# Nine shared fp32 slots, hardware-queue loads and ScalarE casts in a Winograd convolution

## The chip, the cores and the metric

The kernel runs on one core of a Trainium2 chip. The metric is the device time of one execution, in microseconds (us), lower is better. Each number of the form "128.61 us" is the median over several executions. Some executions of the kernel before are slower; an execution more than 1.5% above the fastest of its kernel is called slow, and comparisons use fast executions only. The profile is one fast execution; its span, from the first to the last instruction, is about 2 us shorter than the time of the same execution (125.7 and 127.53 us for the kernel before). In the profile PE is TensorE (matmuls), DVE is VectorE, ACT is ScalarE, POOL is GpSimd, and SP issues the transfers of the sync queue; DMA stands for the sixteen engines that move data between HBM, the large memory, and SBUF, the core's own. PSUM is the memory that the matmuls write to.

## The reference, cut to what matters

A 3x3 convolution, stride 1, padding 1, fp32: 16 images of 64 channels, 64x64 points, to 128 channels.

```python
def setup_inputs():
    batch, c_in, h, w, c_out = 16, 64, 64, 64, 128
    return {"x": np.random.randn(batch, c_in, h, w).astype(np.float32),
            "weight": np.random.randn(c_out, c_in, 3, 3).astype(np.float32) * 0.1}
# reference: x padded by 1; output[b, co] += weight[co, ci, kh, kw] * x_pad[b, ci, kh:kh+h, kw:kw+w]
```

x is 16.8 MB, the output 33.6 MB. All of it must pass through HBM once.

## The kernel before: the parts that matter

Two images (2 x 64 channels) make one "pair" of 128 partitions; there are eight pairs. One pair is 2 MB of fp32 coming in and 2 x 2 MB going out. Along the rows the kernel uses a small Winograd scheme: per block of 16 output rows there is one shared product group U (over sums of two neighbouring rows, `ss`), and two groups A and B (over the rows themselves, `xs`). VectorE adds U to A and to B and so writes the output tiles `ot`. The matmuls want fp16.

```python
    xpool = ctx.enter_context(tc.tile_pool(name="xpool", bufs=5))    # fp16 input pairs, 8 KB a partition
    opool = ctx.enter_context(tc.tile_pool(name="opool", bufs=8))    # fp32 output images, 16 KB
    ...
    nc.sync.dma_start(w_raw, w_flat)
    x0 = opool.tile([128, H, W], F32, tag="ot", name="x0")
    for lo, hi in cuts:                                              # pair 0 comes as fp32, in four pieces
        nc.sync.dma_start(x0[:, lo:hi, :], x_rows[0:128, lo:hi, :])
    ...
    def load(p):                                                     # pairs 1 to 7: the DMA casts to fp16
        xs[p] = xpool.tile([128, H, W], F16, tag="xs", name="xs")
        keep(nc.gpsimd.dma_start(xs[p], x_rows[128 * p : 128 * p + 128, :, :]))
    ...
    for p in range(NP):
        if p + 1 < NP:
            for lo in (0, 16):
                sums(nc.gpsimd, p + 1, xs[p + 1], lo, 16)            # ss of the next pair, on POOL
        ...
        for blk in range(4):
            ...
            U = group([(G1, None)])
            for b2 in range(2):
                keep(nc.scalar.copy(ut, U[b2]))                      # ScalarE: PSUM -> SBUF
            A = group([(G21, 1), (G0, -1)])
            for b2 in range(2):
                nc.vector.tensor_add(ots[b2][:, j0 : j0 + RB, 0, :], A[b2], us[b2])
            Bt = group([(G01, 0), (G2, 2)])
            ...                                                      # the same for the odd rows
            # after block 3 of a pair (pair 7: after blocks 1 and 3): two stores on the sync queue
```

## Time and profile before

| | before |
|---|---|
| time, median of all | 128.61 us (128.06 to 132.51; the last is slow) |
| span of the profile | 125.7 us |
| PE busy | 107.0 us |
| last matmul of the chain of waits ends | 111.84 us |
| HBM read + written | 17.07 + 33.55 = 50.62 MB |
| last data packet ends | 124.3 us |

Lines of the profile's page of the kernel before. The rows under "busy" have one digit for each fortieth of the span (9 = 90% or more busy); GB/s counts bytes after the cast; the queue lines are packets, MB and share of the sixteen DMA engines' time.

```profile
PE 107.0 (85%) x978; PEld 55.9 (44%) x978; DVE 83.7 (67%) x134; ACT 40.8 (32%) x72; POOL 34.8 (28%) x28
...
PE   0489799999999999999999999999999999990000
...
DMA  4999999999999999999999999999999999999980
...
q1 hardware_dynamic: 3312, 35.95, 68.5%
q0 software_dynamic: 1008, 7.34, 28.5%
q8 instruction: 7, 0.11, 0.3%
...
HBM read 17.07 MB, written 33.55 MB: 403 GB/s over the span
```

Three stretches of the same trace, from the view by windows. The columns are start:end, length, then busy time and number of instructions for each engine, then the granted TensorE clock, the DMA share and the GB/s.

```profile
12.00:24.00 12.00, 11.15 (x103) 5.66 (x101) 9.79 (x16) 5.03 (x9) 8.42 (x4) 1.00 1.03 216
...
72.00:88.00 16.00, 16.00 (x154) 8.46 (x152) 12.50 (x21) 5.37 (x10) 4.20 (x2) 1.00 1.01 429
...
96.00:104.00 8.00, 8.00 (x78) 4.25 (x76) 6.67 (x11) 2.15 (x4) 0.00 (x0) 1.00 1.01 430
```

Two engines are full at once here: PE and the DMA. PE's work ends at about 112 us and the transfers go on to 124 us (the end of the last data packet in the trace). From 12 to 24 us only casting loads run (but for the end of pair 0's last piece, which lands at 12.5 us): 216 GB/s of fp16 written is about 432 GB/s of fp32 read. From 72 us on only stores run, at 429 GB/s to 88 us.

### The profile page before, as it was taken

The page shows a single profiled execution, that of the slowest core. Times are in us where ns is not written, and L with a number is a line of the kernel's source. Part 1 is how long each engine was busy: PE and PEld are TensorE (multiplying, and loading weights), DVE is VectorE, ACT ScalarE, POOL GpSimd, SP SyncE. Part 2 cuts the span into 40 slices and gives each one's busy share as a digit, 9 for nine tenths or more (in the row PEclk, how much of TensorE's full clock was granted, in tenths as well). Part 3 has the DMA queues.
Part 4 walks back from the last instruction along what each step waited for, and adds up shares of the span by engine and source line. Part 5 has one row for each costly group of instructions (what it writes and reads, how often), then busy time and mean ns, then how long its engine had stood idle before and what let it go on. Part 6 is the DMA issues. An engine that isn't in the chain of part 4 may idle for free.

```text
span 125.7 us, 2408 instructions
## 1 busy us (share of the span) xinstructions
PE 107.0 (85%) x978; PEld 55.9 (44%) x978; DVE 83.7 (67%) x134; ACT 40.8 (32%) x72; POOL 34.8 (28%) x28
## 2 busy tenths in 40 slices
PE   0489799999999999999999999999999999990000
PEld 0334355555555555555555555555555555540000
DVE  0180798778877777877787778777877787773000
ACT  4283833333333333324333333333333333330000
POOL 2710297893029201930930093000000000000000
PEclk9999999999999999999999999999999999999755
DMA  4999999999999999999999999999999999999980
GB/s 130 325 353 216 224 214 222 211 182 331 326 305 362 315 315 323 422 321 326 307 409 443 433 427 438 417 422 433 427 433 438 417 422 433 427 417 422 422 370 34
DMA packets 4330, 43.43 MB, mean 345 GB/s; under 512 B 480, under 2 KB 480, under 8 KB 1120
## 3 DMA queue, kind: packets, MB, share of 16 engines
q1 hardware_dynamic: 3312, 35.95, 68.5%
q0 software_dynamic: 1008, 7.34, 28.5%
q8 instruction: 7, 0.11, 0.3%
q14 instruction: 3, 0.02, 0.0%
HBM read 17.07 MB, written 33.55 MB: 403 GB/s over the span
## 4 chain that ended last, share of the span: by engine, by line
PE 77%; DMA 8%; ACT 2%; SPq 1%; DVE 1%; issue 1%; DVEq 0%
PE acc L140 77%; DMA x<-in_x_dram 8%; SPq L46 1%; ACT ut L154 1%; ACT xs L94 1%; DVE ot L158 1%; DVEq L195 0%; DVE ot L161 0%; SPq L42 0%; DVEq L158 0%
## 5 line engine op out<-in xcount | busy, mean ns | idle before, releaser
L140 PE MATMUL acc<-xs,Wt 64*128 64x504 f16 (+3 forms) x768 | 95.1, 379 | 0.8 <-ACT ut L154 0.7
L140 PEld LDWEIGHTS <-Wt 64*128 64x128 f16 x960 | 54.8, 96 | 52.4 <-issue 5.1
L158 DVE TENSOR_TENSOR ot<-acc,ut 128x512 f32<-128x512 f32 x64 | 41.2, 686 | 21.2 <-PE acc L140 18.0
L154 ACT COPY ut<-acc 128x512 f32<-128x512 f32 x64 | 34.2, 589 | 64.1 <-issue 59.6
L161 DVE TENSOR_TENSOR ot<-acc,ut 128x512 f32<-128x512 f32 x64 | 41.1, 685 | 0.0
L69 POOL TENSOR_TENSOR ss<-xs 128x1024 f16<-128x1024 f16 x14 | 29.5, 2125 | 23.1 <-DMA xs<-in_x_dram 9.3
L140 PE MATMUL acc<-ss,Wt 64*128 64x504 f16 (+1 forms) x192 | 32.5, 384 | 0.9 <-DVE ss L69 0.9
L69 DVE TENSOR_TENSOR ss<-x 128x512 f16<-128x512 f32 x4 | 2.8, 690 | 9.6 <-DMA x<-in_x_dram 9.6
L56 POOL DMA_DIRECT2D xs<-in_x_dram x7 | 4.0, 575 | 15.8 <-PE acc L140 15.8
L87 PE MATMUL wp<-ident,w 128*64 128x128 f16 x18 | 1.3, 328 | 4.5 <-POOL w L50 4.5
L94 ACT CAST xs<-x 128x1024 f16<-128x1024 f32 (+2 forms) x4 | 4.1, 1052 | 2.4 <-DMA x<-in_x_dram 2.4
L87 PEld LDWEIGHTS <-w 128*64 128x64 f16 x18 | 1.1, 209 | 4.5 <-POOL w L50 4.5
L89 ACT ACT_TABLE_LOAD x1 | 1.3, 1283 | 0.7 <-PEq L184 0.7
L89 ACT CAST Wt<-wp 128x384 f16<-128x384 f32 x1 | 0.5, 480 | 3.1 <-PE wp L87 3.1
L50 POOL CAST w<-w_raw 128x576 f16<-128x576 f32 x1 | 0.7, 662 | 2.5 <-DMA w_raw<-in_weight_dram 2.5
L96 ACT CAST Wt<-wp 128x384 f16<-128x384 f32 x1 | 0.5, 479 | 0.5 <-DVE Wt L92 0.5
L91 DVE TENSOR_TENSOR Wt<-wp,Wt 128x384 f16<-128x384 f32 x1 | 0.6, 550 | 0.0
L92 DVE TENSOR_TENSOR Wt<-wp,Wt 128x384 f16<-128x384 f32 x1 | 0.5, 548 | 0.0
L97 ACT CAST Wt<-wp 128x384 f16<-128x384 f32 x1 | 0.5, 485 | 0.0
masks.py:199 POOL TENSOR_SCALAR_AFFINE_SELECT ident<-ident 128x128 f16<-128x128 f16 x1 | 0.3, 292 | 0.1
masks.py:197 POOL MEMSET ident<- 128x128 f16 x1 | 0.2, 204 | 0.3 <-POOLq L184 0.3
L184 POOL MEMSET const-float32-0.0<- 128x1 f32 x1 | 0.1, 98 | 0.2 <-issue 0.2
(3 smaller groups left out, 0.3 us busy)
## 6 DMA issues: line engine op xcount, KB each, us to landing
out_dram<-ot SPq DMA_DIRECT2D x14, 2048.0 KB, 18.1
xs<-in_x_dram POOLq DMA_DIRECT2D x7, 1024.0 KB, 15.4
out_dram<-ot SPq DMA_DIRECT2D x4, 1024.0 KB, 10.2
x<-in_x_dram SPq DMA_DIRECT2D x2, 512.0 KB, 6.0
x<-in_x_dram SPq DMA_DIRECT2D x1, 576.0 KB, 4.7
x<-in_x_dram SPq DMA_DIRECT2D x1, 448.0 KB, 9.9
w_raw<-in_weight_dram SPq DMA_DIRECT2D x1, 288.0 KB, 3.0
```

The source lines that it names most:

```text
L46: nc.sync.dma_start(x0[:, lo:hi, :], x_rows[0:128, lo:hi, :])
L50: keep(nc.gpsimd.tensor_copy(w16, w_raw))
L56: keep(nc.gpsimd.dma_start(xs[p], x_rows[128 * p : 128 * p + 128, :, :]))
L69: eng.tensor_add(ss[p][:, lo : lo + n, :], v[:, lo : lo + n, 0, :], v[:, lo : lo + n, 1, :])
L87: nc.tensor.matmul(wp[q : q + 64, k * CO : k * CO + CO], w16[:, t::9], ident)
L89: keep(nc.scalar.copy(wrow(G1), wps[1]))
L91: keep(nc.vector.tensor_sub(wrow(G21), wps[2], wrow(G1)))
L94: keep(nc.scalar.copy(xs[0][:, lo:hi, :], x0[:, lo:hi, :]))
L140: nc.tensor.matmul(tiles[b2][:, lo - j0 : hi - j0, c_lo:c_hi], Wt[p0 : p0 + 64, wi, kw, :], rhs, start=i == 0, stop=i == n - 1,)
L154: keep(nc.scalar.copy(ut, U[b2]))
L158: nc.vector.tensor_add(ots[b2][:, j0 : j0 + RB, 0, :], A[b2], us[b2])
L161: nc.vector.tensor_add(ots[b2][:, j0 : j0 + RB, 1, :], Bt[b2], us[b2])
```

## The change

Its intent: all loads come as plain fp32 on the hardware queues; ScalarE, which was idle two thirds of the time, casts to fp16. The fp32 loads (16 KB a partition) and the output images (16 KB) have the same size, so they share nine slots "in turn". Five loads are issued at once, then room is set aside for pair 0's images, and load 5; loads 6 and 7 come later. Cut to its core:

```diff
-    xpool = ctx.enter_context(tc.tile_pool(name="xpool", bufs=5))
-    opool = ctx.enter_context(tc.tile_pool(name="opool", bufs=8))
+    xpool = ctx.enter_context(tc.tile_pool(name="xpool", bufs=3))
+    big = ctx.enter_context(tc.tile_pool(name="big", bufs=9))
...
-    nc.sync.dma_start(w_raw, w_flat)
+    nc.scalar.dma_start(w_raw, w_flat)
...
+    def load(p):
+        xf[p] = big.tile([128, H, W], F32, tag="big", name="xf")
+        for lo, hi in cuts if p == 0 else [(0, H)]:
+            keep(nc.sync.dma_start(xf[p][:, lo:hi, :], x_rows[128 * p : 128 * p + 128, lo:hi, :]))
+    def cast(p, n):                       # one of four pieces
+        ...
+        keep(nc.scalar.copy(xs[p][:, lo:hi, :], xf[p][:, lo:hi, :]))
+    def outs(p):
+        ots[p] = [big.tile([128, H // 2, 2, W], F32, tag="big", name="ot") for _ in range(2)]
+    for p in range(5):
+        load(p)
+    outs(0)
+    load(5)
...
-    keep(nc.gpsimd.tensor_copy(w16, w_raw))
+    keep(nc.vector.tensor_copy(w16, w_raw))
...
+    casts[0] = pieces(1)                  # cast during pair 0
+    casts[1] = pieces(2) + pieces(3)[:2]
+    casts[2] = pieces(3)[2:] + pieces(4)
+    casts[3], casts[4], casts[5] = pieces(5), pieces(6), pieces(7)
...                                        # in each block, after the two copies of U:
+            for q, n in c[len(c) * blk // 4 : len(c) * (blk + 1) // 4]:
+                cast(q, n)
...
+            if blk == 3 and p == 0:
+                outs(1)
+                load(6)
+                outs(2)
+            if blk == 3 and p == 2:
+                load(7)
```

More of the change, by code (lines that the diff above doesn't have):

```diff
@@ L41 @@
     w_raw = const.tile([CO, CI * 9], F32)
-    nc.sync.dma_start(w_raw, w_flat)
-    x0 = opool.tile([128, H, W], F32, tag="ot", name="x0")
+    nc.scalar.dma_start(w_raw, w_flat)
     cuts = [(0, 18), (18, 34), (34, 50), (50, 64)]
-    for lo, hi in cuts:
-        nc.sync.dma_start(x0[:, lo:hi, :], x_rows[0:128, lo:hi, :])
+    xf, xs = {}, {}
+    def load(p):
+        xf[p] = big.tile([128, H, W], F32, tag="big", name="xf")
+        for lo, hi in cuts if p == 0 else [(0, H)]:
+            keep(
+                nc.sync.dma_start(
+                    xf[p][:, lo:hi, :], x_rows[128 * p : 128 * p + 128, lo:hi, :]
+                )
+            )
+    def cast(p, n):
+        if p not in xs:
+            xs[p] = xpool.tile([128, H, W], F16, tag="xs", name="xs")
+        lo, hi = cuts[n]
+        keep(nc.scalar.copy(xs[p][:, lo:hi, :], xf[p][:, lo:hi, :]))
+    ots = {}
+    def outs(p):
[4 more added lines that the diff above has]
+    load(5)
     ident = const.tile([128, 128], F16)
@@ L49 @@
     w16 = const.tile([CO, CI * 9], F16)
-    keep(nc.gpsimd.tensor_copy(w16, w_raw))
-    xs = {0: xpool.tile([128, H, W], F16, tag="xs", name="xs")}
-    def load(p):
-        xs[p] = xpool.tile([128, H, W], F16, tag="xs", name="xs")
-        keep(nc.gpsimd.dma_start(xs[p], x_rows[128 * p : 128 * p + 128, :, :]))
-    for p in range(1, 5):
-        load(p)
+    keep(nc.vector.tensor_copy(w16, w_raw))
     ss = {}
@@ L89 @@
     keep(nc.scalar.copy(wrow(G1), wps[1]))
-    sums(nc.vector, 0, x0, 0, RB)
+    sums(nc.vector, 0, xf[0], 0, RB)
     keep(nc.vector.tensor_sub(wrow(G21), wps[2], wrow(G1)))
     keep(nc.vector.tensor_sub(wrow(G01), wps[0], wrow(G1)))
-    for n, (lo, hi) in enumerate(cuts):
-        keep(nc.scalar.copy(xs[0][:, lo:hi, :], x0[:, lo:hi, :]))
-        if n == 0:
-            keep(nc.scalar.copy(wrow(G0), wps[0]))
-            keep(nc.scalar.copy(wrow(G2), wps[2]))
-        if n < 3:
-            sums(nc.vector, 0, x0, RB * (n + 1), RB)
-    for p in range(NP):
-        if p + 1 < NP:
-            for lo in (0, 16):
-                sums(nc.gpsimd, p + 1, xs[p + 1], lo, 16)
-        if p > 0 and p + 4 < NP:
-            load(p + 4)
-        ots = [
-            opool.tile([128, H // 2, 2, W], F32, tag="ot", name="ot") for _ in range(2)
-        ]
+    cast(0, 0)
+    keep(nc.scalar.copy(wrow(G0), wps[0]))
+    keep(nc.scalar.copy(wrow(G2), wps[2]))
+    for n in range(1, 4):
+        sums(nc.vector, 0, xf[0], RB * n, RB)
+    pieces = lambda q: [(q, n) for n in range(4)]
+    casts = {p: [] for p in range(NP)}
+    casts[0] = pieces(1)
+    casts[1] = pieces(2) + pieces(3)[:2]
+    casts[2] = pieces(3)[2:] + pieces(4)
+    casts[3], casts[4], casts[5] = pieces(5), pieces(6), pieces(7)
+    assert NP == 8
+    for p in range(NP):
+        if p not in ots:
+            outs(p)
+        for q, _ in dict.fromkeys((q, 0) for q, _ in casts[p]):
+            if q not in ss:
+                for lo in (0, 16):
+                    sums(nc.gpsimd, q, xf[q], lo, 16)
         for blk in range(4):
@@ L155 @@
                 us.append(ut)
+            if p == 0 and blk < 3:
+                cast(0, blk + 1)
+            c = casts[p]
+            for q, n in c[len(c) * blk // 4 : len(c) * (blk + 1) // 4]:
+                cast(q, n)
             A = group([(G21, 1), (G0, -1)])
             for b2 in range(2):
-                nc.vector.tensor_add(ots[b2][:, j0 : j0 + RB, 0, :], A[b2], us[b2])
+                nc.vector.tensor_add(ots[p][b2][:, j0 : j0 + RB, 0, :], A[b2], us[b2])
             Bt = group([(G01, 0), (G2, 2)])
             for b2 in range(2):
-                nc.vector.tensor_add(ots[b2][:, j0 : j0 + RB, 1, :], Bt[b2], us[b2])
+                nc.vector.tensor_add(ots[p][b2][:, j0 : j0 + RB, 1, :], Bt[b2], us[b2])
+            if blk == 3 and p == 0:
[4 more added lines that the diff above has]
+                load(7)
             parts = {3: (0, 64)} if p < NP - 1 else {1: (0, 32), 3: (32, 64)}
@@ L165 @@
                 for b2 in range(2):
-                    nc.sync.dma_start(
+                    keep(nc.sync.dma_start(
                         out_rows[2 * p + b2, :, lo:hi, :],
-                        ots[b2].rearrange("p j i c -> p (j i) c")[:, lo:hi, :],
-                    )
+                        ots[p][b2].rearrange("p j i c -> p (j i) c")[:, lo:hi, :],
+                    ))
 _INS = ['x', 'weight']
```

## The prediction

> **What bounds the kernel now.** The chain of waits is 77% PE, but it stops at 113.8 us of a 125.7 us span; the rest is waiting for stores. The DMA row is at 9 from the second slice to the thirty-eighth. The queue table gives 68.5% (hardware queue) plus 28.5% (software queue): 97% of all sixteen engines' time. The software queue's 7.34 MB are counted after the cast; the HBM line says 17.07 MB read and 33.55 MB written, 50.6 MB in all. Windows with stores alone (72 to 112 us) move 429 GB/s; the Trainium skill, "DMA: Bandwidth & Descriptors", section "Where 436 GB/s comes from", puts the ceiling at 435, which this trace supports. So the transfers bound this kernel; PE (about 97 us of steady work) hides behind them with about 4 us to spare.
>
> **What the change does.**
> - Bytes over HBM stay at 50.6 MB. Casting in the DMA saved none: with casting loads alone (12 to 24 us) the queue delivered 216 GB/s of fp16, 432 of fp32 read. The skill's section "Issuing engines are not separate DMA queues" says all queues end on the same 16 engines; the mixed window (24 to 64 us) agrees: 422 GB/s of source bytes.
> - Packets: a casting 16 KB row took 624 ns alone and up to 686 among stores (mean about 637). Plain loads in 4096 and 3584 byte packets took 159 and 140 ns; that line extends to about 615 ns for 16 KB. 896 packets x 22 ns / 16 engines = 1.2 us saved. Stores: 620 ns among casts, 613 alone: 0.3 us.
> - Start: from 2.5 to 12 us the before kernel read at only about 384 GB/s, and x0 shared the engines with casts and landed at 12.5 us. Now x0 heads one queue: it should land near 8 us. About 0.5 us of transfer time, and PE's stall at 12.6 to 14.0 us goes.
> - ScalarE gains 28 casts, 7 x 4.1 = 29 us: busy 41 to about 70 us. In pair 0 that is nearly 12 us in a 12.2 us pair: tight, but PSUM buffers it.
> - POOL loses 4 us of issues; its sums now read fp32, off the path.
> - Slots: the second image of pair 2 reuses the slot of load 3, whose last cast sits behind the copies of block 1 of pair 2. VectorE must wait, and PE loses about 1.7 us near 38 us. Pair 3 reuses pair 0's image slots, whose stores land near 50 us, just when wanted. PE's last store is issued near 115 us, while the transfers have backlog until about 117. So this should not show in the time.
>
> **Result.** Saved on the bound: 1.2 + 0.3 + 0.5 = 2.0 us; the span goes from 125.7 to about 123.7, the time to about 127.0 us (1.4% less). 80% range 125.6 to 129.0. Faster by over 2%: 0.24; within 2%: 0.70; slower: 0.06.
>
> **What would show it.** DMA row at 9 throughout, near 425 GB/s from the second slice on; load packets near 615 ns; one hardware queue near 97%; ScalarE near 70 us; a VectorE wait on a ScalarE cast at the start of pair 2; the last stores landing after a backlog.
>
> **What would make it wrong.** A hole in the DMA row: a late slot holds up ready stores behind it in the one queue. PE losing over 4 us to slots and casts. Plain loads as slow as 4 KB packets (412 GB/s): nothing saved.

## The result, and the profile after

The changed kernel took **136.91 us** (136.18 to 137.95, four executions, all fast) against 128.61 us (128.06 to 132.51, the last one slow): the ratio is 1.067, with a 95% interval of 1.057 to 1.077. (Ratios here are the mean time of one kernel's fast executions over that of the other's from the same rounds, so they are not quite the ratio of the medians that I quote.) It is slower, and outside my range.

The page of the changed kernel, the lines that answer to those shown before, and the row of the granted clock:

```profile
PE 108.5 (81%) x978; PEld 54.6 (41%) x978; DVE 84.2 (63%) x135; ACT 67.1 (50%) x100; POOL 33.5 (25%) x20
...
PE   0099799999995109999999999999999999998000
...
PEclk9999999999999955999999999999999999999965
DMA  4999999999999999999995999199739955999993
...
q1 hardware_dynamic: 4176, 50.33, 88.8%
...
HBM read 17.07 MB, written 33.55 MB: 377 GB/s over the span
```

There are two new things. PE has a hole in slices 13 to 15 (about 40 to 50 us), with the clock at half after it. And the DMA row, which was full before, has holes from about 72 us on, some 25 us after PE's hole. The longest waits (engine, line, what it waited for: us in total, times, longest) name the hole:

```profile
DVE ot L184 <- DMA out_dram<-ot: 10.8, 2, 6.7
...
PE acc L161 <- DVE ot L184: 8.0, 2, 4.5
```

And the timeline from 37 to 54 us (start, length, engine, line, operation, and in brackets the idle time before it and what ended it) shows it happen:

```profile
37.47 2.87 PE L161 MATMUL acc<-xs,Wt 64*128 64x512 f16 x24
...
38.98 0.67 SPq L52 DMA_DIRECT2D xf<-in_x_dram  x1
...
45.04 0.69 DVE L184 TENSOR_TENSOR ot<-acc,ut 128x512 f32<-128x512 f32 x1 [6.68 <-DMA out_dram<-ot]
45.78 0.37 PE L161 MATMUL acc<-xs,Wt 64*128 64x512 f16 x1 [3.50 <-DVE ot L184]
49.89 0.69 DVE L184 TENSOR_TENSOR ot<-acc,ut 128x512 f32<-128x512 f32 x1 [4.16 <-DMA out_dram<-ot]
50.50 1.28 DVE L187 TENSOR_TENSOR ot<-acc,ut 128x512 f32<-128x512 f32 x2
50.63 2.71 PE L161 MATMUL acc<-xs,Wt 64*128 64x512 f16 x11 [4.48 <-DVE ot L184]
...
53.69 2.96 PE L161 MATMUL acc<-xs,Wt 64*128 64x512 f16 x24
```

The first sum of pair 2 waits until pair 0's first image has been stored (45.04 us), the second until its second image has (49.89 us). PE in turn waits for VectorE's sums, for 3.50 and 4.48 us. After that 11 matmuls take 2.71 us, 246 ns each, where at full clock 24 take 2.96 us, 123 ns each. The Trainium skill, "TensorE: Matmul & The Clock Gate", part 1 on the clock gate, says that after an idle window of about 3.4 us the array's clock falls back to half. This trace agrees: the granted clock was 0.50 from 46.5 to 53.3 us. It fell 0.35 us into the second idle stretch, so it was the first, of 3.50 us, that it followed. The view by windows, inside that time:

```profile
48.00:52.00 4.00, 1.37 (x8) 0.61 (x9) 2.11 (x4) 0.00 (x0) 0.00 (x0) 0.50 0.98 422
```

Why did pair 2 wait for pair 0's stores? My forecast had pair 2's images in the slots of loads 2 and 3. The addresses of the tiles in the built programs, one line for each of the nine slots, in order of use (x3 is load 3; 2a and 2b are pair 2's two images), show that the compiler did not deal the slots in turn:

```
changed kernel             the good slots (my forecast's places for pairs 2 and 3)
x0  1a  3a  6b             x0  1a  4b
x1  1b  4a                 x1  1b  5b
x2  x7                     x2  2a  6a
x3  3b  7a                 x3  2b  6b
x4  4b                     x4  x7  7a
0a  2a  5a                 0a  3a  7b
0b  2b  5b                 0b  3b
x5  6a                     x5  4a
x6  7b                     x6  5a
```

Pair 2's images stand in pair 0's image slots. The slot of load 2, whose last cast ended at 33.2 us, was given to load 7 instead, which nothing reads before pair 5. Load 6 got a fresh slot, and so was issued at the very start, with the other loads. The right-hand table is not the strict turn either: in turn, pair 1's images would have had the ninth slot and that of load 0, load 6 that of load 1, and pairs 4 and 5 would differ accordingly. It keeps the compiler's places for pair 1 and load 6, and pairs 2 and 3 stand where I had read them. The strict turn was not run.

The other half of the story is where pair 0's stores stood. They were issued at 25.0 us, but in the same queue behind loads 0 to 6, 14.7 MB, of which only 8.9 MB had moved by 24 us. The Trainium skill, "DMA: Bandwidth & Descriptors", section "Queues, rings and completion order", says that on each DMA engine descriptors of a ring are consumed in ring order. This trace agrees: what was issued on this queue landed in the order of issue, load 6 at 40.0 us and the two stores at 44.9 and 49.8. So the stores' 4.2 MB came last, and landed 20 and 24 us after their issue.

The accounts: the chain's last matmul ends at 122.43 us against 111.84, 10.6 us later. Of this the wait is 8.0, the half clock about 1.4 (2.71 us less 11 x 0.123), and a later start 0.8 (pair 0's stores are issued at 24.98 us against 24.21); 0.4 us are left over. The span grew by 8.7 us only.

### The profile page after: what moved, and what is told of

It is laid out like the page before. It is cut to its first block, busy times and chain, and to the rows that moved or that the text cites. A ratio compares the mean times of both kernels' runs of the same rounds, so it can differ in the third digit from the quotient of the medians.

```text
span 134.4 us, 2438 instructions
## 1 busy us (share of the span) xinstructions
PE 108.5 (81%) x978; PEld 54.6 (41%) x978; DVE 84.2 (63%) x135; ACT 67.1 (50%) x100; POOL 33.5 (25%) x20
## 4 chain that ended last, share of the span: by engine, by line
PE 58%; DMA 18%; DVE 3%; ACT 1%; issue 1%; DVEq 0%
PE acc L161 58%; DMA out_dram<-ot 18%; DVE ot L184 2%; DVE ot L187 1%; ACT xs L61 1%; DVEq L227 0%; ACT ut L175 0%; DVEq L184 0%
## 5 line engine op out<-in xcount | busy, mean ns | idle before, releaser
L161 PE MATMUL acc<-xs,Wt 64*128 64x504 f16 (+3 forms) x768 | 96.8, 382 | 8.8 <-DVE ot L184 8.0
L161 PEld LDWEIGHTS <-Wt 64*128 64x128 f16 x960 | 53.4, 96 | 62.2 <-issue 13.8
L184 DVE TENSOR_TENSOR ot<-acc,ut 128x512 f32<-128x512 f32 x64 | 41.3, 686 | 33.2 <-PE acc L161 18.7
L85 POOL TENSOR_TENSOR ss<-xf 128x1024 f16<-128x1024 f32 x14 | 32.8, 2367 | 53.6 <-issue 34.2
L61 ACT CAST xs<-xf 128x1024 f16<-128x1024 f32 (+2 forms) x32 | 33.2, 1058 | 2.7 <-DMA xf<-in_x_dram 2.7
L75 DVE CAST w<-w_raw 128x576 f16<-128x576 f32 x1 | 0.5, 459 | 6.1 <-DMA w_raw<-in_weight_dram 6.1
L85 DVE TENSOR_TENSOR ss<-xf 128x512 f16<-128x512 f32 x4 | 2.6, 683 | 0.0
```

Source lines behind the costliest of these rows:

```text
L61: keep(nc.scalar.copy(xs[p][:, lo:hi, :], xf[p][:, lo:hi, :]))
L75: keep(nc.vector.tensor_copy(w16, w_raw))
L85: eng.tensor_add(ss[p][:, lo : lo + n, :], v[:, lo : lo + n, 0, :], v[:, lo : lo + n, 1, :])
L161: nc.tensor.matmul(tiles[b2][:, lo - j0 : hi - j0, c_lo:c_hi], Wt[p0 : p0 + 64, wi, kw, :], rhs, start=i == 0, stop=i == n - 1,)
L184: nc.vector.tensor_add(ots[p][b2][:, j0 : j0 + RB, 0, :], A[b2], us[b2])
```

## The experiments

Theory: the time was lost in one wait, made of two things together: pair 2's images in pair 0's slots, and pair 0's stores behind the loads in one queue. Rivals: the ScalarE casts are too much (they add 26 us of busy time), plain loads move less, or one queue is worse than two whatever the slots.

### Slots written out: the good ones, and the compiler's own as a control

The pool of nine becomes nine tags of one buffer each, and a table says which tile gets which. All instructions keep their order on every engine.

```diff
-    big = ctx.enter_context(tc.tile_pool(name="big", bufs=9))
+    big = ctx.enter_context(tc.tile_pool(name="big", bufs=1))
+    XS = [0, 1, 2, 3, 4, 7, 8, 4]                                          # control: [0, 1, 2, 3, 4, 7, 8, 2]
+    OS = [(5, 6), (0, 1), (2, 3), (5, 6), (7, 0), (8, 1), (2, 3), (4, 5)]
+    # control: [(5, 6), (0, 1), (5, 6), (0, 3), (1, 4), (5, 6), (7, 0), (3, 8)]
-        xf[p] = big.tile([128, H, W], F32, tag="big", name="xf")
+        xf[p] = big.tile([128, H, W], F32, tag=f"b{XS[p]}", name="xf")
-        ... tag="big", name="ot") for _ in range(2)]
+        ... tag=f"b{n}", name="ot") for n in OS[p]]
```

> The changed kernel with each tile's slot written out, so that pair 2's images take the slots of loads 2 and 3 instead of those of pair 0's images. Same instructions, same order, same queue. Theory (slot assignment): the changed kernel lost its time because pair 2's first sums waited for pair 0's stores to land at 45 and 50 us. With that wait gone, PE idle before pair 2 falls from 8.0 us to under 2.5 us (what is left is the wait for load 3's last cast), and the time is 126 to 129 us. Rival (ScalarE casts, or plain loads, or the single queue cost the time by themselves): it stays at 135 us or more.

> Control: slots written out exactly as the compiler had given them in the changed kernel (pair 2's images on pair 0's). If the way of writing slots is neutral: 135 to 138 us, two VectorE waits on pair 0's stores of together about 11 us. If the writing itself matters, it moves away from that and the first run can't be read.

Measured: good slots **127.75 us** (127.65 to 127.82), ratio to the kernel before 1.002 (0.994 to 1.009). Control **136.77 us**, ratio 1.073 (1.061 to 1.085), with VectorE waits on pair 0's stores of 11.6 us:

```profile
DVE ot L186 <- DMA out_dram<-ot: 11.6, 2, 7.4
```

So the way of writing is neutral, and the slot table alone is worth 9 us: all of the loss. With it the casts, the plain loads and the single queue together cost nothing against the kernel before that these runs can resolve (the interval reaches from 0.6% faster to 0.9% slower), and the rivals fall. In the kernel with good slots, the one wait that is left at pair 2 is the one I had forecast, on load 3's last cast:

```profile
42.22 0.69 DVE L186 TENSOR_TENSOR ot<-acc,ut 128x512 f32<-128x512 f32 x1 [2.00 <-ACT xs L63]
```

It costs nothing that can be seen: the page lists 0.1 us of idle time before PE's main groups of matmuls, and the chain's last matmul ends at 112.10 us.

### Bad slots, but the stores earlier in the queue

```diff
     outs(0)
-    load(5)
...
                 outs(1)
-                load(6)
                 outs(2)
...          # after pair 0's two stores:
+                if p == 0:
+                    load(5)
+                    load(6)
```

(on top of the control)

> Slots as bad as in the control, but loads 5 and 6 are issued behind pair 0's stores, so that 8.4 MB instead of 12.6 or 14.7 MB stand ahead of those stores in the queue. Theory (the stores stood behind the loads in one queue): the stores land about 10 us earlier, near 35 and 40 us, the wait at pair 2 shrinks to under 2 us, time 127 to 130 us. Rival (the slot sharing is bad wherever the stores stand): the wait stays over 5 us and the time over 133 us.

(The 8.4 MB in this text leave out load 0; the five loads ahead of the stores are 10.5 MB.)

Measured: **128.03 us** (127.64 to 128.32), ratio 1.004. Both VectorE waits on stores in this kernel, from its timeline:

```profile
40.86 0.69 DVE L185 TENSOR_TENSOR ot<-acc,ut 128x512 f32<-128x512 f32 x1 [1.74 <-DMA out_dram<-ot]
...
55.44 1.29 DVE L185 TENSOR_TENSOR ot<-acc,ut 128x512 f32<-128x512 f32 x2 [4.80 <-DMA out_dram<-ot]
```

At pair 2 the wait is down to 1.74 us, as expected: with the slots unchanged, the place in the queue alone repairs it. It takes both things to lose the time. A new wait of 4.80 us appears at pair 3, whose first image has the slot of pair 1's first. It is not that pair 1's stores are later: the same 18.9 MB (loads 0 to 6 and pair 0's stores) stand ahead of them, and the first lands at 55.3 us, against 54.6 us in the changed kernel. There pair 3 came only after 60 us, delayed by the wait before; here it is on time and meets the next shared slot. I had not foreseen it. PE ends at 114.47 us, 2.6 us later than before, and the time hardly shows it; the next two runs say why.

### Is there anything to gain behind the wait?

With good slots I had forecast 2 us less than before, and there were none. First, PE's small losses were tidied up:

```diff
-    nc.scalar.dma_start(w_raw, w_flat)
+    nc.sync.dma_start(w_raw, w_flat)
-    casts[1] = pieces(2) + pieces(3)[:2]
-    casts[2] = pieces(3)[2:] + pieces(4)
+    casts[1] = pieces(2) + pieces(3)[:3]
+    casts[2] = pieces(3)[3:] + pieces(4)
```

(on top of the good slots)

> The first run (good slots) with load 3's third piece cast in pair 1, so that its last cast comes in block 0 of pair 2, and with the weights first on the sync queue instead of on ScalarE's. If transfers bound the kernel once the slot wait is gone, it equals the first run within 1 us although PE ends 2 to 3 us earlier: 126 to 128 us. If PE's losses still count, it is 2 us or more faster than the first run.

Measured: **127.74 us**, the same as the good slots' 127.75. It is a weak test, though, since PE did not end earlier: 112.51 us. The waits at pair 2 went, but the first cast of load 1 stands in ScalarE's order in block 0 of pair 0 and held the copies behind it for 4.4 us, until load 1 landed at 15.0 us. It stands there in the good slots' kernel too, with a wait of 2.8 us.

So the opposite test: take a third of PE's work away, in the kernel before, in the good slots and in the control. Their outputs are wrong, which doesn't matter for the times.

```diff
-                    for kw in (1, 0, 2):
+                    for kw in (1, 0):
-                n = 3 * len(wi_rows)
+                n = 2 * len(wi_rows)
```

> The kernel before with a third of the matmuls left out (one of the three column taps; the result is wrong on purpose), so that VectorE, at about 11 us a pair instead of PE's 12.2, paces the work and each pair's stores are ready earlier. If transfers bound the kernel before: within 1% of it. If PE does: 5 us or more faster.

> The same cut in the changed kernel with good slots (wrong result on purpose). It measures the bound of the new transfers without PE's help or harm, beside the run before it. If plain loads cheapen the transfers by 2 us as I forecast from packet times, it is 1.5 to 2 us faster than the cut kernel before. If only the bytes count (the bytes moved by a given time in the two traces differ by 0.3 MB at most), 0 to 1 us.

> The same cut with the changed kernel's own (bad) slots, wrong result on purpose. The wait for pair 0's stores still ends near 50 us, but afterwards a pair takes 11 us, not 12.2. If the late 9 us were lost because PE came late with the last pairs' stores and the queue ran dry, most of them come back: 127 to 131 us, and the holes in the DMA row after 72 us shrink. If the slots cost in another way, it stays over 134 us.

| | whole, median us | cut, median us | cut over before |
|---|---|---|---|
| kernel before | 128.90 (these rounds, slow executions included; the fast ones 127.21 to 128.90) | 126.63 | 0.992 (0.989 to 0.996) |
| good slots | 127.75 | 126.55 | 0.992 (0.989 to 0.995) |
| the changed kernel's slots | 136.77 | 126.63 | 0.993 (0.989 to 0.997) |

(The whole kernels of the second and third rows ran in earlier rounds, on another chip. The last column compares fast executions of the same rounds, so it is not the quotient of the two before it.) Two results follow.

First, casting loads and plain loads have the same bound: 126.63 and 126.55 us. The traces agree: where casting loads brought about 432 GB/s of fp32 (12 to 24 us, above), plain loads brought 431 in the kernel with good slots:

```profile
12.00:24.00 12.00, 11.92 (x108) 5.70 (x106) 9.04 (x15) 8.59 (x12) 9.30 (x4) 1.00 1.01 431
```

The 2 us that I had forecast to be saved on the transfers are 0.1 us.

Second, the changed kernel's bad wait costs nothing when PE and VectorE can catch up. The cut control still waits, and still its DMA row stays full and its time is that of the good slots. Its largest wait on a transfer, and its DMA row:

```profile
DVE ot L186 <- DMA out_dram<-ot: 10.5, 1, 10.5
...
DMA  3999999999999999999999999999999999999970
```

So the time of the changed kernel was not lost at 40 to 50 us, when the wait occurred; the transfers were full then. It was lost from 72 us on, when the queue had caught up with a PE that was late for good. These are stretches of the changed kernel:

```profile
60.00:72.00 12.00, 12.00 (x116) 6.08 (x112) 9.21 (x16) 8.09 (x13) 3.89 (x2) 1.00 1.01 429
72.00:88.00 16.00, 16.00 (x155) 8.15 (x151) 12.62 (x21) 10.12 (x15) 7.61 (x4) 1.00 0.72 306
...
96.00:104.00 8.00, 8.00 (x78) 4.11 (x76) 5.92 (x11) 3.65 (x7) 0.00 (x0) 1.00 0.66 279
```

and the same stretches with good slots:

```profile
60.00:72.00 12.00, 12.00 (x116) 6.36 (x114) 9.19 (x16) 7.71 (x12) 4.58 (x2) 1.00 1.01 427
72.00:88.00 16.00, 16.00 (x154) 8.50 (x152) 12.46 (x21) 9.97 (x15) 4.69 (x2) 1.00 1.00 427
...
96.00:104.00 8.00, 8.00 (x80) 4.24 (x76) 6.42 (x11) 2.15 (x4) 0.00 (x0) 1.00 0.94 399
```

PE is full in all of them. It is the DMA share that falls, to 0.72 and 0.66 in the changed kernel, and, a little, to 0.94 from 96 to 104 us even with good slots, where pair 6's stores are issued (101.31 us) while the queue is running empty: from 101 to 102 us the share is 0.52.

### An attempt to beat both

```diff
+            at = (0, 0, 1, 3, 4) if p == 0 else [len(c) * i // 4 for i in range(5)]
-            for q, n in c[len(c) * blk // 4 : len(c) * (blk + 1) // 4]:
+            for q, n in c[at[blk] : at[blk + 1]]:          # pair 1's casts not in block 0 of pair 0
-            parts = {3: (0, 64)} if p < NP - 1 else {1: (0, 32), 3: (32, 64)}
+            parts = {3: (0, 64)} if p < NP - 3 else {1: (0, 32), 3: (32, 64)}
```

(on top of the tidied kernel)

> Good slots, load 3's last cast early, weights first on sync, pair 1's casts not before block 1 of pair 0 (in the runs so far the first of them held ScalarE until load 1 landed at 14 us), and the stores of the last three pairs in halves. PE should end 1.5 to 3 us earlier than in the tidied run (about 110 us) and the gap in the transfers near 101 us should close. If transfers bound, the time is only 0 to 1 us under the tidied run's, 126.5 to 127.7 us. If PE still counts, 125 to 126.

Measured: **128.21 us** (127.80 to 128.66), ratio to the kernel before 1.005 (1.001 to 1.008): a miss, outside my expectation. PE did end earlier (110.75 us) and the hole at 101 us is gone (share 1.01 from 96 to 104 us), and yet it is not faster than the tidied kernel, which had 1.002 (0.994 to 1.010) in its own rounds. Its last stretches, by windows, PE and all engines long idle:

```profile
122.00:123.00 1.00, 0.00 (x0) 0.00 (x0) 0.00 (x0) 0.00 (x0) 0.00 (x0) 0.50 0.24 98
123.00:124.00 1.00, 0.00 (x0) 0.00 (x0) 0.00 (x0) 0.00 (x0) 0.00 (x0) 0.50 0.06 25
124.00:126.00 2.00, 0.00 (x0) 0.00 (x0) 0.00 (x0) 0.00 (x0) 0.00 (x0) 0.50 0.04 16
```

A share of 0.06 is one engine of sixteen. In the packets, from 122.6 us on, each starts 0.31 us after the one before and takes 0.31 us, to the last at 125.4 us: they come one after the other, as from a single engine that lags, for 2.8 us. With good slots it is 1.8 us (122.8 to 124.6).

### What lags at the end

In the cut kernels that tail is 0.6 to 1.2 us, and the instruction queue of the page has five packets, in the full ones seven: fewer matmuls, fewer instructions to fetch. The rule is not clean, though: the kernel before has seven too, and its tail is only 0.8 us. So: good slots, PE's third tap kept as an instruction but shrunk to one column, beside a repeat of the cut kernel.

```diff
-                    for kw in (1, 0, 2):
+                    for kw in (1, 2, 0):
+                            if kw == 2:
+                                hi, c_hi = lo + 1, c_lo + 1
+                                rhs = rhs[:, 0:1, 0:1]
```

> Good slots, the third column tap kept as an instruction but shrunk to one column (wrong result on purpose), so that PE has as many instructions as in the full kernel and nearly as little work as in the cut one. In the full kernels seven 16 KB fetches of instructions pass through the DMA engines and the last packets then come one after the other for about 2 us, as if one engine lagged; the cut kernels have five fetches and about 1 us of such a tail. If the instruction fetches make that tail, this kernel has seven fetches again and is about 1 us slower than the cut kernel run beside it, though PE is far ahead. If PE's work was what the cut took away, it equals the cut kernel.

> The cut kernel with good slots once more, as the neighbour of the run before: 126.3 to 126.9 us, five instruction fetches, last packets about 1 us behind the others.

Measured: with the tiny tap **127.39 us** (127.27 to 127.54), without **126.40 us** (126.27 to 126.61): 1.0 us apart, ranges far from touching. Both have PE finished by 97 us. The instruction queue and the stretch from 123 to 124 us, with the tiny tap,

```profile
q8 instruction: 7, 0.11, 0.3%
...
123.00:124.00 1.00, 0.00 (x0) 0.00 (x0) 0.00 (x0) 0.00 (x0) 0.00 (x0) 0.50 0.06 25
```

and without:

```profile
q8 instruction: 5, 0.08, 0.2%
...
123.00:124.00 1.00, 0.00 (x0) 0.00 (x0) 0.00 (x0) 0.00 (x0) 0.00 (x0) 0.50 0.00 0
```

So the number of instructions sets part of the end of the transfers, with PE's work no longer in the way: the two runs differ in instruction count (320 small matmuls and their weight loads) and in a tiny amount of PE work. That also corrects the reading of the cut kernels: about 1 us of what they gained probably came from fewer instructions, not from less PE work; it was tested with good slots alone. The comparison among the three cut kernels stands, since all have five fetches.

A lagging engine would also explain why holes in the transfers are forgiven up to about 2 us: while the others wait for work, the lagging engine catches up. The kernel with bad slots and early stores has a DMA share of only 0.88 from 96 to 112 us, but it still moves about 430 GB/s from 122 to 124 us, has a tail of only 0.6 us, and so ends like the rest. The trace does not say which engine a packet ran on, so that it is one engine, and the one that fetches instructions, is argued and not shown. Nor is it settled why the tails differ so much with the same seven fetches: 0.8 us in the kernel before, 1.8 with good slots, 2.8 in the last attempt. An engine that is slow for another reason is a rival that no run here tests.

## Why the prediction was wrong, point by point

- **"So the transfers bound this kernel": right.** The kernel before with a third of PE's work gone is within 1% of itself (126.63 us, ratio 0.992), and the last pair of runs suggests that most of that 1% goes with the instruction count.
- **"Slots: the second image of pair 2 reuses the slot of load 3 ... Pair 3 reuses pair 0's image slots": wrong, and this is the step that failed.** I dealt the nine slots in turn, in program order, as the kernel's words say. The built program gave pair 2 the slots of pair 0's images. In place of a wait of 1.7 us on a cast came waits of 10.8 us on stores, and PE lost 8.0 us and 1.4 more at half clock. With pairs 2 and 3 in the slots that I had read, the time is 127.75 us, inside my range and 0.75 us from my 127.0; but that closeness is luck, since the kernel before ran faster in those rounds (127.45 us) and the ratio to it is 1.002, not the 1.4% less that I forecast. The addresses were in the built program before the run; I looked at the order of instructions only.
- **"PE's last store is issued near 115 us ... So this should not show in the time": right for the slots I had in mind, but with less to spare than the 4 us I claimed.** With good slots the queue began to run empty at about 101 us although PE was only 0.3 us later than before (112.10 and 111.84 us). In the changed kernel PE's 10.6 us went far beyond that, and the holes from 72 us on are the loss.
- **"A late slot holds up ready stores behind it in the one queue" and "PE losing over 4 us to slots": the second is the danger that came true, the first not.** It was the reverse: stores stood behind loads that had slots too early.
- **"Saved on the bound: 1.2 + 0.3 + 0.5 = 2.0 us": wrong in size, by nearly all of it.** The packet times came out as forecast (a median of 611 ns for 16 KB rows on the hardware queue), but the 1.5 us of packet time were not time. The packets of the casting queue overlapped: their share was 1.03 where they ran alone, and they brought as many bytes in a stretch as plain loads (about 432 and 431 GB/s). Here the bytes were what counted. Summing packet sizes of the traces, with casting loads counted at their fp32 size, 3.71 MB had been moved after 12 us in the kernel before and 3.74 MB with good slots: the start gave 0.03 MB, 0.07 us at 430 GB/s, not 0.5. After 60 us it was 23.93 and 24.25 MB, a lead of 0.32 MB or 0.75 us; after 104 us, past the hole at 101 us, 0.14 MB of the lead were left (42.69 and 42.83 MB). The cut kernels, without the hole, show 0.1 us.
- **"PE's stall at 12.6 to 14.0 us goes": wrong.** Pair 0's load landed at 9.5 us, sooner than before (12.5) but not near 8. The weights, moved to ScalarE's queue, shared the engines with pair 0's first piece and landed at 6.1 us instead of 3.8; and ScalarE waited in order for load 1 in block 0.
- **ScalarE near 70 us busy: right** (67.1), and harmless. POOL's sums on fp32: 2.37 us each instead of 2.13, harmless too.

## What to carry to other kernels

A pool that serves tiles of different lifetimes does not promise an order: before you argue about what a tile waits for, read the addresses in the built program, and where the order matters write it out, one tag to a slot. A store that frees a slot stands behind every load already in its queue, so a load issued early into a free slot can cost a wait much later; look where the next user of a slot stands in the queue. And when two resources are nearly full, judge savings on transfers by bytes moved by a given time, not by summed packet times, and look for the loss where the full resource runs empty (here 72 us) rather than where the wait occurred (here 40 us).

## What the Trainium skill lacked or had wrong

- "DMA: Bandwidth & Descriptors", section "Issuing engine by pattern", says that hardware queues are generally faster than the software queue. For 2 MB loads in 16 KB rows, in kernels that the transfers bound, they were not: 126.55 us with plain loads on the hardware queue and 126.63 us with casting loads on the software queue, both with PE out of the way.
- The same page, section "Where 436 GB/s comes from", warns that between HBM and SBUF the HBM side, about 358 GB/s, binds. With this one core running, 427 GB/s were sustained from 60 to 88 us with good slots, near the page's 435. The warning needs the condition, which the page gives elsewhere, that both cores of a pair are busy.
- "Runtime: NRT & Kernel Launch", section "Instruction fetch mechanics", says nothing of a cost to the kernel's own transfers. Here a kernel with seven fetches of 16 KB took 1.0 us longer than one with five, both bound by the transfers (127.39 against 126.40 us); that the fetches are the cause is argued above, not shown.
- No page that I read warns that packet times of a queue can overlap so that their sum is not time ("DMA: Bandwidth & Descriptors", section "Two DMAs through the same engine are not ordered", comes nearest): a share of 1.03 in the windows of casting loads, and a "saving" of 1.5 us that was 0.1 us.
- No page that I read says how a pool of slots is dealt out, which here was not in program order: 9 us (136.77 against 127.75 us).
